# Read-back order and the start of z's job in a one-core block with two linear-attention branches

## The chip, the cores and the metric

The kernel runs on one core of a Trainium2 chip. The metric is the device time of one execution in microseconds (us), as the median of several runs; less is better.

## The reference

One layer, sequence 256, model width 2048, all in float32. From the normalised and modulated input h a wide projection gives the inputs of two branches, and their results are merged, projected and followed by a gated feed-forward block:

```
h    = rms_norm(x) * (1 + scale_m) + shift_m          # 256 x 2048; scale, shift from c @ ada_w
proj = h @ w_in                                       # q,k,v,o of branch A; q|k|v, z of branch B; gates
# branch B: 16 heads of 128, both directions, chunks of 64, gated delta rule
a_mat = I + beta_i * (k k^T) * decay_strict           # per chunk, unit lower triangular
t_mat = inverse(a_mat)                                # triangular solve
u, w  = t_mat @ (beta v), t_mat @ (beta exp(g) k)
...                                                   # recurrence over the chunks -> o_b
y_b   = (rms_norm(o_b) * silu(z)) @ w_branch_b
x     = x + gate_m * ((g_a*y_a + g_b*y_b) @ w_out)
x     = x + gate_f * SwiGLU(norm(x)) ; out = rms_norm(x)
```

## The kernel before

Every large product is made from split weights. A weight tile `raw` (128 x 2048, 1 MB) is loaded by the SyncE queue; ScalarE copies half of it rounded to fp32r (`wh`, 128 x 1024), VectorE makes the rest (`wl = raw - wh`), and TensorE sums three products, `wh*hh`, `wh*hl` and `wl*hh` (`hh`, `hl` are the same split of h). There are three buffers each of `raw`, `wh` and `wl`. A job (`tjob` for 512 columns, `fjob` for 128) is a generator that yields after each half tile; `fill(n)` takes n steps of the jobs that wait in the list `fills`, so that TensorE has work while branch B's small chains run. In the names below, `wl_z1_2_0` is the wl of z's job for group 1, load 2, half at 0; one half is 12 matmuls of TensorE.

Branch B's 16 heads go in four groups of four (`GRP`). `gdn_phase1(h)` computes a head's gates and decays (`dec`, scans over `al`, the decays loaded from HBM by `decay_load`), and on VectorE the triangles `mi`, `mb` from TensorE's products `ks`. GpSimd stores the 32 x 32 diagonal blocks of `mi` to HBM (four DMAs into `inst_d`) and reads them back rearranged into the rows of `uu`. When the fourth head of a group has been read back, `gdn_invert` inverts all 64 blocks of the group at once on VectorE, 60 instructions in place (`utmp` and `uu`), with a `fill(1)` every few of them; GpSimd stores the inverse to HBM and loads it again as `cg`, from which `gdn_blocks` makes `R` and `X`. `gdn_phase2` uses them for two heads at a time: its first product is `p<-R`, its last transposes are `px`, which ScalarE evicts to `obt`.

The four groups run one after the other. While group g is in phase 2, the projections and phase 1 of group g+1 run in `stream`. At the end of a group, z's job of the next group (`z_job(g + 1)`, 8 halves) is put ahead of the other jobs, and `invert(g + 1)` begins. I call these ends the first, second and third turn: about 435 to 515 us (z1, uu1, head 7), 630 to 705 us (z2, uu2, head 11) and 820 to 895 us (z3, uu3, head 15). Group 0 has its z job before.

What sets the order: each engine and each DMA queue works strictly down its own list, and the framework makes these lists from the program with a scheduler. Instructions wrapped in `order(...)` keep their place in the program among each other; others may be taken earlier or later. In `tjob`, the argument `early` is the number of halves that are split before the job's first products, and wherever it is not 0, all `wh` and `wl` of that job are wrapped in `order`. DMAs of GpSimd are on GpSimd's list, with the small `memset` of `al`.

Of the kernel before, what the change touches and what calls it, by code (L numbers as in the profile page):

```python
# [21 lines left out]
NH_B, DK_B = 16, 128  # L22
# [3 lines left out]
GRP = 4  # L26
# [26 lines left out]
def hybrid_block(ctx: ExitStack, tc: tile.TileContext, xr, nfr, crow, pk_d, cst_d, ada2, ada4, win0, winb, wint, wba, wbb, wo, wgu, wd, out, dbg=None):  # L53
# [3 lines left out]
    def pool(stack, name, bufs=1, **kw):  # L57
        return stack.enter_context(tc.tile_pool(name=name, bufs=bufs, **kw))
# [12 lines left out]
    def order(ins, yes=True):  # L71

        return tc.keep_in_program_order(ins) if yes else ins
# [33 lines left out]
    def add():  # L107

        part, b, raw = asked.pop(0)
        c = part * KB + b  # L110
        order(V.scalar_tensor_tensor(raw, raw, 1.0, row_c[:, :D], ALU.mult, ALU.mult, accum_out=mod[:, c : c + 1]), room[0][3] > 1)  # L111
        if b == KB - 1:
            c = slice(part * KB, part * KB + KB)
            V.tensor_tensor(mod[:, c], mod[:, c], pk[:, PK_ADAB + c.start : PK_ADAB + c.stop], ALU.add)
# [31 lines left out]
    def settle(keep=0, only=None):  # L146

        now = [f for f in behind if only is None or f.__name__ == only]
        for f in now[: len(now) - keep]:
            behind.remove(f)  # L150
            f()
# [111 lines left out]
    fills = []  # L263

    def fill(n=1):

        while n and fills:
            if next(fills[0], None):
                n -= 1
            else:  # L270
                fills.pop(0)
# [26 lines left out]
    heads, parts = {}, {}  # L298
# [11 lines left out]
    def decay_load(h):  # L310
        al = als[h] = fr.tile([P, 2, T + 8], F32, tag="al", bufs=2, name=f"al{h}")
        order(G.memset(al[:, :, 0:8], 0.0))
        order(G.dma_start(al[:, :, 8:], alpha_d[:, h].partition_broadcast(P)))
# [48 lines left out]
    def z_job(g, early=0):  # L362
        def done(ps):
            szs[g] = evp.tile([P, 2, 512], F32, tag="sz", bufs=1, name=f"sz{g}")
            for t in range(2):
                S.activation(szs[g][:, t], ps[t], AF.Silu)
        return tjob(f"z{g}", [wint[g, u] for u in range(4)], hh, hl, done, early)
# [121 lines left out]
    with ExitStack() as s0:  # L489
# [72 lines left out]
        zj = z_job(0, 3)  # L562
# [20 lines left out]
    def gdn_phase1(h):  # L583
# [62 lines left out]
        g, hl_ = divmod(h, GRP)  # L646
# [5 lines left out]
                inst[4 * b : 4 * b + 4].rearrange("x j i -> j x i"), mi[32 * b : 32 * b + 32, :, 32 * b : 32 * b + 32]  # L652
            ), b)

        if h + 2 < NH_B:
            decay_load(h + 2)
        order(G.dma_start(uus[g][16 * hl_ : 16 * hl_ + 16], inst))

        cc = ccs[h % NB]

# [43 lines left out]
    def gdn_blocks(g):  # L704

        cg = bk.tile([P, 2, 512], F32, tag="uu", bufs=1, name=f"cg{g}")
        for b in range(4):
            G.dma_start(cg[32 * b : 32 * b + 32, 0], inv_d[g][:, b].rearrange("j x i -> j (x i)"))
        yield
        order(V.transpose(cg[:, 1], cg[:, 0]))  # L710
        F_, Bt, Ft, B_ = (cg[:, i // 2, (i % 2) * 256 : (i % 2 + 1) * 256].rearrange("p (m c) -> p m c", m=8) for i in range(4))

        def mix(dst, a, ca, b, cb):
            order(V.tensor_scalar(dst, b, cb, None, ALU.mult))
            order(V.scalar_tensor_tensor(dst, a, ca, dst, ALU.mult, ALU.add))

        mix(R[:, 0], Ft, even, Bt, odd)
        mix(R[:, 1], B_, even, F_, odd)
        yield
        for i, ab in enumerate(((Ft, Bt), (B_, F_))):  # L720
            for b in range(4):
                r = slice(32 * b, 32 * b + 32)
                order(S.activation(X[r, i, :, b % 2], ab[b // 2][r], AF.Copy))
            yield
        for i, a in enumerate((F_, B_)):
            for b in range(4):
                r = slice(32 * b, 32 * b + 32)
                if i:
                    order(V.tensor_copy(UL[r, i, :, r], a[r]))
                else:  # L730
                    order(S.activation(UL[r, i, :, r], a[r], AF.Copy))
            yield
# [139 lines left out]
    def stream(h0):  # L872

        todo = []

        def piece():

            for q in list(todo):
                q[0] -= 1
                if not q[0]:  # L880
                    todo.remove(q)
                    next(heads1[q[1]])

        for h in range(h0, min(h0 + 2, NH_B)):
            for j in range(3):
                for _ in b_job(h, j):
                    piece()
                    yield True
            todo += [[2, h], [4, h]]
        while todo:  # L890
            fill(1)
            piece()
            yield True
        while True:
            fill(1)
            yield True
# [3 lines left out]
    def mlstm(h):  # L900
# [84 lines left out]
        yield  # L985

    heads1 = {h: gdn_phase1(h) for h in range(NH_B)}
    after = (0, 1, 2, 1, 2, 2, 2, 2, 4, 0)
    last = (0, 1, 2, 1, 2, 2, 1, 1, 3, 0)
# [13 lines left out]
    def invert(g):  # L1003
        gen = gdn_invert(g)
        next(gen)
        fill(4 if g else 6)
        for _ in gen:
            fill(1)

    invert(0)  # L1010
    for g in range(4):
        blocks = gdn_blocks(g)
        next(blocks)
        fill(8)
        next(blocks)
        fill(1)
        pairs = [gdn_phase2(g, p) for p in range(2)]
        if g == 3:
            settle()
            sf.close()  # L1020
            mq["pool"] = pool(sq_, "mq", side="right")
            first2 = [mlstm(h) for h in range(2)]
            for c in first2:
                next(c)
        every[0] = (4, 2, 2, 2)[g]
        for p in range(2):
            pieces = stream(4 * g + 2 * p + 4)
            for n in range(1, 10):

                held[0] = n < 4  # L1030
                if p == 0:
                    next(blocks, None)
                if n == 9 and p and g < 3:

                    zj = z_job(g + 1, int(4 * g + 7 in heads))
                    if 4 * g + 7 in heads:
                        next(zj)
                next(pairs[p], None)
                if g == 3 and n == (8, 4)[p]:
                    next(first2[p])  # L1040
                for _ in range(last[n] if g == 3 else second[n] if p else after[n]):
                    next(pieces)
            for _ in pairs[p]:
                pass

            if g < 3:
                while 4 * g + 2 * p + 5 not in heads:
                    next(pieces)
        if g < 3:
            fills.insert(0, zj)  # L1050
            every[0] = owed[0] = 0
            if asked:
                add()
            invert(g + 1)
# [483 lines left out]
```

## Time and profile before

| | |
|---|---|
| three runs | 2067.28 us median, 2060.01 to 2068.92 |
| profiled execution | 2064.07 us, span 2062.1 us |
| granted TensorE clock, mean | 0.993 |
| TensorE busy | 2019.9 us |
| VectorE / ScalarE / GpSimd busy | 1397.8 / 1027.7 / 116.8 us |
| branch B, heads and groups | from about 160 to 1000 us of the span |

A busy TensorE is the rule throughout, so the views to read are the waits of TensorE, and what each of the three turns looks like on the engines that feed it. "Idle before" in a row is the time in which that engine stood, and behind the arrow is what ended it.

### The profile page before, as it was taken

The numbers are of one execution on the slowest core, as the hardware profiler recorded it, in microseconds if no ns is written. First come the engines' busy times: TensorE is split into PE (matmuls) and PEld (weight loads), VectorE is DVE, ScalarE is ACT, GpSimd is POOL, SyncE is SP. The second block draws the span as 40 slices with busy tenths as digits, with TensorE's granted clock in tenths as the row PEclk, the third lists the DMA queues.
The fourth block names the chain that finished last, engine by engine and source line by source line (L and its number), as shares of the span: only waits on it lengthen the run. The fifth ranks groups of instructions, "written<-read, shape, count | busy, mean of one in ns | idle before, by whom it ended". The sixth has DMA issues, their size and how long they took to land.

```text
span 2062.1 us, 27024 instructions
## 1 busy us (share of the span) xinstructions
PE 2019.9 (98%) x10386; PEld 1697.9 (82%) x10386; DVE 1397.8 (68%) x2062; ACT 1027.7 (50%) x1540; POOL 116.8 (6%) x211
## 2 busy tenths in 40 slices
PE   8999999999999999999999999999999999999998
PEld 6878789978997889789787888788888888878886
DVE  5778877867878788866577778756565655455554
ACT  3146647755665577454534444644444444444443
POOL 0001210111001010110100000200000000000000
PEclk9999999999999999999999999999999999999999
DMA  9986666646666767586776878466766665555553
GB/s 401 420 334 208 193 228 225 215 124 218 227 206 207 241 213 244 189 291 250 258 278 249 321 283 296 157 232 232 255 225 226 251 237 184 187 201 191 197 189 137
DMA packets 78962, 485.64 MB, mean 236 GB/s; under 512 B 10585, under 2 KB 15969, under 8 KB 24433
## 3 DMA queue, kind: packets, MB, share of 16 engines
q1 hardware_dynamic: 63360, 450.95, 60.4%
q0 software_dynamic: 8160, 17.88, 4.0%
q10 hardware_dynamic: 7314, 15.10, 1.9%
q8 instruction: 81, 1.33, 0.3%
q14 instruction: 47, 0.39, 0.1%
HBM read 467.07 MB, written 16.82 MB: 235 GB/s over the span
## 4 chain that ended last, share of the span: by engine, by line
PE 85%; DMA 6%; DVE 6%; ACT 1%; issue 1%; POOL 0%; ACTq 0%; SPq 0%; DVEq 0%; POOLq 0%
PE acc_gt L230 4%; PE acc_gt L232 4%; PE acc_gt L231 4%; PE acc_up L232 4%; PE acc_up L230 4%; PE acc_up L231 4%; PE acc_d L231 4%; PE acc_d L230 4%; PE acc_d L232 4%; DMA ra<-ada 3%; PE acc_o L230 3%; PE acc_o L232 3%; PE acc_o L231 3%; PE acc_b L187 2%; PE acc_b L188 2%; PE acc_b L189 2%
## 5 line engine op out<-in xcount | busy, mean ns | idle before, releaser
L211 DVE TENSOR_TENSOR wl_d<-raw_d,wh_d 128x1024 fp32r<-128x1024 f32 x88 | 107.8, 1225 | 119.9 <-ACT wh_d L209 119.9
L211 DVE TENSOR_TENSOR wl_up<-raw_up,wh_up 128x1024 fp32r<-128x1024 f32 x88 | 107.7, 1225 | 111.3 <-ACT wh_up L209 111.2
L211 DVE TENSOR_TENSOR wl_gt<-raw_gt,wh_gt 128x1024 fp32r<-128x1024 f32 x88 | 108.1, 1229 | 89.2 <-ACT wh_gt L209 89.2
L187 PE MATMUL acc_b<-hh,wh_b 128*128 128x256 f32 x576 | 164.8, 286 | 0.0
L209 ACT ACTIVATE wh_d<-raw_d 128x1024 fp32r<-128x1024 f32 x88 | 93.3, 1061 | 138.9 <-PE acc_d L231 134.0
L189 PE MATMUL acc_b<-hh,wl_b 128*128 128x256 f32 x576 | 160.9, 279 | 0.0
L188 PE MATMUL acc_b<-hl,wh_b 128*128 128x256 f32 x576 | 159.7, 277 | 0.0
L209 ACT ACTIVATE wh_gt<-raw_gt 128x1024 fp32r<-128x1024 f32 x88 | 93.3, 1060 | 128.7 <-PE acc_gt L231 77.3
L111 DVE SCALAR_TENSOR_TENSOR ada<-ada,crow 128x2048 f32<-128x2048 f32 x64 | 146.1, 2282 | 10.2 <-DMA ada<-ada 10.2
L209 ACT ACTIVATE wh_up<-raw_up 128x1024 fp32r<-128x1024 f32 x88 | 93.2, 1060 | 118.1 <-PE acc_up L231 84.2
L230 PE MATMUL acc_gt<-wh_gt,hfh 128*128 128x512 f32 x352 | 139.0, 395 | 0.0
L231 PE MATMUL acc_gt<-wh_gt,hfl 128*128 128x512 f32 x352 | 138.2, 393 | 0.0
L232 PE MATMUL acc_gt<-wl_gt,hfh 128*128 128x512 f32 x352 | 137.4, 390 | 0.0
L230 PE MATMUL acc_up<-wh_up,hfh 128*128 128x512 f32 x352 | 136.9, 389 | 0.0
L231 PE MATMUL acc_up<-wh_up,hfl 128*128 128x512 f32 x352 | 136.9, 389 | 0.0
L232 PE MATMUL acc_up<-wl_up,hfh 128*128 128x512 f32 x352 | 136.9, 389 | 0.0
L230 PE MATMUL acc_d<-wh_d,ffh 128*128 128x512 f32 x344 | 134.3, 391 | 0.0
L231 PE MATMUL acc_d<-wh_d,ffl 128*128 128x512 f32 x344 | 134.3, 390 | 0.0
L232 PE MATMUL acc_d<-wl_d,ffh 128*128 128x512 f32 x344 | 133.9, 389 | 0.0
L557 PE MATMUL first<-x,raw 128*128 128x256 f32 x512 | 115.9, 386 | 6.3 <-ACT x L551 6.3
L557 PEld LDWEIGHTS first<-x,raw 128*128 128x128 f32 x512 | 97.3, 192 | 25.0 <-ACT x L551 11.9
L187 PEld LDWEIGHTS acc_b<-hh,wh_b 128*128 128x128 f32 x576 | 108.5, 188 | 1.2 <-issue 0.9
(373 smaller groups left out, 5261.3 us busy)
## 6 DMA issues: line engine op xcount, KB each, us to landing
ada<-ada SPq DMA_DIRECT2D x64, 1024.0 KB, 5.0
raw_gt<-wgu SPq DMA_DIRECT2D x44, 1024.0 KB, 4.9
raw_up<-wgu SPq DMA_DIRECT2D x44, 1024.0 KB, 4.9
raw_d<-wd SPq DMA_DIRECT2D x44, 1024.0 KB, 4.8
raw_b<-winb SPq DMA_DIRECT2D x36, 1024.0 KB, 5.1
ra<-ada SPq DMA_DIRECT2D x32, 1025.0 KB, 15.2
raw<-win SPq DMA_DIRECT2D x16, 1024.0 KB, 14.5
raw_z<-wint SPq DMA_DIRECT2D x16, 1024.0 KB, 5.4
```

The costliest lines, as they stand in the source:

```text
L111: order(V.scalar_tensor_tensor(raw, raw, 1.0, row_c[:, :D], ALU.mult, ALU.mult, accum_out=mod[:, c : c + 1]), room[0][3] > 1)
L187: PE.matmul(o, wh[:, k], hh[:, kk], start=kk == 0, stop=False)
L188: PE.matmul(o, wh[:, k], hl[:, kk], start=False, stop=False)
L189: PE.matmul(o, wl[:, k], hh[:, kk], start=False, stop=kk == KB - 1)
L209: order(S.activation(wh, raws[u][:, k0 : k0 + 2], AF.Copy), early)
L211: order(V.tensor_tensor(wl, raws[u][:, k0 : k0 + 2], wh.bitcast(F32), ALU.subtract), early)
L230: order(PE.matmul(ps[t], xh[:, kk, c], wh[:, k], start=kk == 0, stop=False), early and steps > 1)
L231: PE.matmul(ps[t], xl[:, kk, c], wh[:, k], start=False, stop=False)
L232: PE.matmul(ps[t], xh[:, kk, c], wl[:, k], start=False, stop=kk == last)
L557: PE.matmul(first[o], raw[:, o], x[:, b], start=b == 0 and o % 2 == 0, stop=b == KB - 1 and o % 2 == 1)
```

## The change

Two edits. For the last head of a group, GpSimd's DMA that reads the triangles back into `uu` is put ahead of the memset and DMA that load the decays of the head after next (heads 3, 7 and 11; the last head, 15, loads no decays any more). And z's job is no longer started ahead of its turn: before, `zj` was made at step 9 of the second pair with `early` 1 and its first `next` split the first half; now it is made when it is put into `fills`, with `early` 0, so it splits its first weights itself, and its `wh` and `wl` are no longer wrapped in `order`.

```diff
@@ gdn_phase1
-        if h + 2 < NH_B:
+        final = hl_ == GRP - 1
+        if h + 2 < NH_B and not final:
             decay_load(h + 2)
         order(G.dma_start(uus[g][16 * hl_ : 16 * hl_ + 16], inst))
+        if h + 2 < NH_B and final:
+            decay_load(h + 2)
@@ loop over the groups
-                if n == 9 and p and g < 3:
-
-                    zj = z_job(g + 1, int(4 * g + 7 in heads))
-                    if 4 * g + 7 in heads:
-                        next(zj)
                 next(pairs[p], None)
@@
         if g < 3:
-            fills.insert(0, zj)
+            fills.insert(0, z_job(g + 1))
             every[0] = owed[0] = 0
```

What it moves in the engines' lists, at three places. On GpSimd at the first turn (`inst_d1`, `uu1`: store and read-back of head 7's triangles; `al9`: decays of head 9), before and after:

```order
L651 DMA inst_d1_119<-mi7_3700 32x4x32 x4
L312 MEMSET al9_3723 128x2x8
L313 DMA al9_3723<-alpha_d_92 128x2x256
L657 DMA uu1_2779<-inst_d1_119 16x1024
L681 DMA inv_d1_123<-uu1_2779 16x16x32 x8
```
```order
L651 DMA inst_d1_119<-mi7_3700 32x4x32 x4
L658 DMA uu1_2779<-inst_d1_119 16x1024
L312 MEMSET al9_3724 128x2x8
L313 DMA al9_3724<-alpha_d_92 128x2x256
L684 DMA inv_d1_123<-uu1_2779 16x16x32 x8
```

The read-back moved ahead of the memset and the decay load, and nothing else changes on GpSimd; groups 0 and 2 look alike.

On VectorE at the first turn, from the last of head 7's triangles to the start of the inversion (`dec8`: decays of head 8), before, and then after, from the sums that precede the triangles:

```order
L645 STREAM_TRANSPOSE mi7_3700<-mb7_3701 128x256
L211 TENSOR_TENSOR wl_z1_0_0_3730<-raw_z1_0_3727,wh_z1_0_0_3729 128x1024
...
L211 TENSOR_TENSOR wl_z1_0_2_3765<-raw_z1_0_3727,wh_z1_0_2_3764 128x1024
L211 TENSOR_TENSOR wl_z1_1_0_3783<-raw_z1_1_3780,wh_z1_1_0_3782 128x1024
L211 TENSOR_TENSOR wl_z1_1_2_3799<-raw_z1_1_3780,wh_z1_1_2_3798 128x1024
L593 SCALAR_TENSOR_TENSOR dec8_4611<-al8_3487,cst_75 128x128
L684 MEMSET uu1_2779 64x32
...
L695 TENSOR_TENSOR uu1_2779<-uu1_2779,utmp1_3749 64x27x4
L211 TENSOR_TENSOR wl_z1_2_0_3826<-raw_z1_2_3823,wh_z1_2_0_3825 128x1024
```
```order
L211 TENSOR_TENSOR wl_z1_0_0_3743<-raw_z1_0_3740,wh_z1_0_0_3742 128x1024
...
L211 TENSOR_TENSOR wl_z1_0_2_3765<-raw_z1_0_3740,wh_z1_0_2_3764 128x1024
L211 TENSOR_TENSOR wl_z1_1_0_3783<-raw_z1_1_3780,wh_z1_1_0_3782 128x1024
L635 SCALAR_TENSOR_TENSOR mi7_3700<-ks7_0_3704,sm7_3690,dec7_3641 128x128
...
L645 STREAM_TRANSPOSE mi7_3700<-mb7_3701 128x256
...
L211 TENSOR_TENSOR wl_z1_1_2_3799<-raw_z1_1_3780,wh_z1_1_2_3798 128x1024
L593 SCALAR_TENSOR_TENSOR dec8_4611<-al8_3487,cst_75 128x128
L211 TENSOR_TENSOR wl_z1_2_0_3826<-raw_z1_2_3823,wh_z1_2_0_3825 128x1024
L211 TENSOR_TENSOR wl_z1_2_2_3848<-raw_z1_2_3823,wh_z1_2_2_3847 128x1024
L687 MEMSET uu1_2779 64x32
```

Three of z's wl moved ahead of the triangles, and the fifth and sixth ahead of the inversion's first instruction. ScalarE's wh moved with them: the first three stand ahead of `obt` and of the copies `cc` of the triangles, where before it was one.

On ScalarE at the third turn (`vv15`: scaled values of head 15; `obt`: eviction of group 2's last transposes; `cc3`: copies of the triangles), before and after:

```order
L621 ACTIVATE vv15_7668<-vps15_7589,nn15_7662 128x128
L209 ACTIVATE wh_z3_0_0_7697<-raw_z3_0_7695 128x1024
L664 ACTIVATE cc3_1163<-mi15_7671 32x2x32
...
L830 ACTIVATE obt10_7711<-px_2_1_7531,pk_74 128x256
L830 ACTIVATE obt11_7714<-px_2_1_7531,pk_74 128x256
...
L209 ACTIVATE wh_z3_0_2_7733<-raw_z3_0_7695 128x1024
```
```order
L621 ACTIVATE vv15_7668<-vps15_7589,nn15_7662 128x128
L833 ACTIVATE obt10_7699<-px_2_1_7531,pk_74 128x256
L833 ACTIVATE obt11_7702<-px_2_1_7531,pk_74 128x256
...
L209 ACTIVATE wh_z3_0_0_7711<-raw_z3_0_7709 128x1024
L667 ACTIVATE cc3_1163<-mi15_7671 32x2x32
...
L209 ACTIVATE wh_z3_0_2_7733<-raw_z3_0_7709 128x1024
```

Here z's first wh moved the other way, behind both `obt`. At the second turn the first three wh stand ahead of `obt` as at the first, and the second and third wl come right behind the first, ahead of the scans `dec`.

## The prediction

> **What bounds the kernel now.** I read the page first, then the list of what TensorE waits for, then the stretches in which it waits. The first row below is the page's busy time, the others the whole run's waits (us in total, times, longest).
>
> ```profile
> PE 2019.9 (98%) x10386; PEld 1697.9 (82%) x10386; DVE 1397.8 (68%) x2062; ACT 1027.7 (50%) x1540; POOL 116.8 (6%) x211
> ...
> PE acc_z L232 <- DVE wl_z L211: 9.8, 10, 2.5
> ...
> PE acc_z L230 <- ACT wh_z L209: 1.7, 2, 0.9
> ```
>
> TensorE is busy for 98%, so the end moves only by its waits and by its clock. Its largest wait is for z's split weights, 11.5 us in all, and the change touches just these. The next table goes by stretches around the first turn (z1) and, last row, the third (z3).
>
> ```profile
> core 0: us, PE busy (x) PEld busy (x) DVE busy (x) ACT busy (x) POOL busy (x), PEclk, DMA share, GB/s
> ...
> 443.00:446.40 3.40, 1.50 (x7) 1.24 (x7) 3.40 (x8) 3.33 (x8) 2.35 (x6) 1.00 0.32 91
> 446.40:449.80 3.40, 3.40 (x9) 2.61 (x8) 3.40 (x4) 1.20 (x2) 1.11 (x2) 0.50 0.59 53
> ...
> 456.60:460.00 3.40, 0.91 (x5) 0.43 (x4) 3.13 (x11) 1.06 (x1) 0.00 (x0) 1.00 0.17 70
> 460.00:463.40 3.40, 3.40 (x9) 2.62 (x10) 3.22 (x8) 0.00 (x0) 0.00 (x0) 0.51 0.00 0
> ...
> 825.00:828.70 3.70, 2.19 (x10) 1.14 (x8) 3.70 (x12) 3.23 (x10) 0.74 (x2) 1.00 0.11 35
> ```
>
> After a stretch in which TensorE worked 1.50 or 0.91 of 3.40 us, its granted clock is 0.50 and 0.51 for the next 3.4 us. That costs 3.4 x (0.50 + 0.49) = 3.4 us on top of the idle time. After 2.19 of 3.70 us it stayed at full speed.
>
> **First turn (z1): why it waits.** TensorE, VectorE and ScalarE in order of time (start us, us; in brackets the idle time before):
>
> ```profile
> 439.31 0.39 PE L231 MATMUL acc_mb<-wh_mb,hl 128*128 128x512 f32 x1
> ...
> 441.84 0.48 PE L230 MATMUL acc_z<-wh_z,hh 128*128 128x512 f32 x1
> ...
> 444.92 0.73 PE L232 MATMUL acc_z<-wl_z,hh 128*128 128x512 f32 x2 [1.90 <-DVE wl_z L211]
> ...
> 459.82 0.60 PE L232 MATMUL acc_z<-wl_z,hh 128*128 128x512 f32 x1 [2.49 <-DVE wl_z L211]
> ...
> 513.49 0.97 PE L746 MATMUL p<-R,cc 128*128 128x32 f32 x8
> ```
> ```profile
> 440.83 0.35 DVE L635 SCALAR_TENSOR_TENSOR mi<-ks,sm,dec 128x128 f32<-128x128 f32 x1 [4.44 <-PE ks L630]
> ...
> 443.68 1.18 DVE L211 TENSOR_TENSOR wl_z<-raw_z,wh_z 128x1024 fp32r<-128x1024 f32 x1
> ...
> 456.60 0.17 DVE L689 TENSOR_TENSOR utmp<-uu 64x30 f32<-64x30 f32 x1 [6.52 <-issue]
> ...
> 458.56 1.21 DVE L211 TENSOR_TENSOR wl_z<-raw_z,wh_z 128x1024 fp32r<-128x1024 f32 x1
> ...
> 466.12 0.37 DVE L689 TENSOR_TENSOR utmp<-uu 64x220 f32<-64x220 f32 x1
> 466.52 0.38 DVE L695 TENSOR_TENSOR uu<-uu,utmp 64x220 f32<-64x220 f32 x1
> ...
> 491.37 0.18 DVE L695 TENSOR_TENSOR uu<-uu,utmp 64x30 f32<-64x30 f32 x1
> ...
> 506.95 0.48 DVE L715 SCALAR_TENSOR_TENSOR R<-cg,cst,R 128x256 f32<-128x256 f32 x1
> ```
> ```profile
> 435.17 1.05 ACT L209 ACTIVATE wh_z<-raw_z 128x1024 fp32r<-128x1024 f32 x1
> 442.12 0.84 ACT L830 ACTIVATE obt<-px,pk 128x256 f32<-128x256 f32 x2 [5.89 <-PE px L826]
> ...
> 453.93 1.06 ACT L209 ACTIVATE wh_z<-raw_z 128x1024 fp32r<-128x1024 f32 x1 [1.69 <-PE acc_z L231]
> 456.68 1.06 ACT L209 ACTIVATE wh_z<-raw_z 128x1024 fp32r<-128x1024 f32 x1 [1.69 <-PE acc_z L231]
> ```
>
> z's first wl stood behind head 7's triangles and came at 443.68. The wait of 2.49 us has another cause: VectorE stood 6.52 us until the triangles had been read back into uu, and z's fifth wl was queued behind that (456.60, then 458.56).
>
> **First turn after the change.** ScalarE and VectorE now split z's first three half loads before the triangles, in time that stood idle (5.89 and 4.44 us). The third needs the buffer that `mb` frees at 439.31 + 0.39 = 439.7: wh to 440.8, wl to 442.0. So the triangles start 1.2 us later than at 440.83; that is the price. The wait of 1.90 us goes. z's fifth and sixth wl stand ahead of uu now and need only buffers that TensorE frees: the 2.49 us go too, and with both the half clock. Removed: 4.4 + 3.4 = 7.8 us.
>
> What is late next? TensorE then needs a new split pair each 2.75 us (453.93 to 456.68) from 441.84 on without a pause. The read-back decides where VectorE's inversion stands. The GpSimd rows, and the times from issue to landing of four read-backs (of 447.97, 641.89, 832.07 and 810.30, in this order):
>
> ```profile
> 446.27 0.73 POOL L313 DMA_DIRECT2D al<-alpha_d  x1
> 447.97 0.52 POOL L657 DMA_DIRECT2D uu<-inst_d  x1 [0.97 <-DMA inst_d<-mi]
> ...
> 832.07 0.51 POOL L657 DMA_DIRECT2D uu<-inst_d  x1 [1.95 <-DMA inst_d<-mi]
> ```
> ```profile
> uu<-inst_d POOLq DMA_DIRECT2D x1, 64.0 KB, 8.6
> ...
> uu<-inst_d POOLq DMA_DIRECT2D x1, 64.0 KB, 6.3
> ...
> uu<-inst_d POOLq DMA_DIRECT2D x1, 64.0 KB, 5.3
> ...
> uu<-inst_d POOLq DMA_DIRECT2D x1, 64.0 KB, 3.6
> ```
>
> The read-back is not issued sooner by its new place: it waits for the store of the triangles (0.97 us even behind the decay load, 1.95 without one). The gain is in the landing: 8.6 and 6.3 us with the decay load in front, 5.3 and 3.6 for heads 15 and 14, which have none. I take 5.3, because the next weight load (`raw_mb`) will run beside it as `raw_z` did at 832; bounds 3.6 and 8.6. Hence uu at 447.97 + 1.2 + 5.3 = 454.5 instead of 456.6. The decay load then lands some 4 us later and nobody waits: head 9 reads it a group later.
>
> By the Trainium skill (DMA: Bandwidth & Descriptors, Queues, rings and completion order) each DMA engine goes round-robin between queue rows, a packet at a time. The trace agrees for the read-backs beside a 1 MB load, which still land in 5.3 us; that rule alone would leave 5.3 where it is.
>
> From 454.5 I count VectorE's rows in the new order, 0.42 us for a long inversion step (466.12 to 466.52) and 1.13 for a wl. Most wl are in time. Twice nine steps stand between two wl, 3.8 us against 2.75: ahead of `wl_mb1_3_0` TensorE waits about 0.8 us, ahead of `wl_o1_1_0` 0.5. So 7.8 - 1.3 = 6.5 us are left. The inversion ends near 489.3 (one wl fewer in it), 2 us before 491.4, so R's first half comes near 505 instead of 507.4; TensorE comes to p at 513.5 - 6.5 = 507.0. It passes, with 2 us to spare. Bounds: 7.8 us, and 2.0 with the landing at 8.6, when the wl queued behind uu are 3.3 us late and a half-clock stretch may return.
>
> **Second turn (z2).** Waits between 625 and 670 us, then a piece of the chain:
>
> ```profile
> PE acc_z L230 <- ACT wh_z L209: 1.7, 2, 0.9
> PE acc_z L232 <- DVE wl_z L211: 1.2, 3, 0.5
> ```
> ```profile
> 642.99 7.49 DMA raw_z<-wint
> ```
>
> 2.9 us. The third load of z2 could start only when `wl_z2_0_2` had freed its buffer (642.99). That wl now comes right behind the first, near 639.9, so the load lands 3 us sooner. Given back: about 0.4 at `wl_z2_2_0`, behind uu, and 1.3 where nine inversion steps stand ahead of `wl_ma2_2_2`. Net 1.2 us, bounds 0 and 2.9.
>
> **Third turn (z3).** No decay load here; only the order of ScalarE differs, and it is worse at the start.
>
> ```profile
> PE acc_z L232 <- DVE wl_z L211: 3.2, 4, 1.6
> ```
> ```profile
> 824.92 1.05 ACT L209 ACTIVATE wh_z<-raw_z 128x1024 fp32r<-128x1024 f32 x1
> ```
> ```profile
> 825.39 0.60 PE L826 MATMUL px<-cst,on 128*128 128x128 f32 x4
> ...
> 828.82 0.73 PE L232 MATMUL acc_z<-wl_z,hh 128*128 128x512 f32 x2 [1.60 <-DVE wl_z L211]
> ```
>
> wh_z3_0_0 ran at 824.92, ahead of obt. Now it stands behind both obt, which wait for px (to 826.0): obt to 827.1, wh to 828.2, wl to 829.3. TensorE stands from 826.0 to 828.2 and comes to its first wl 0.6 us later than at 828.82. The other three waits (3.2 - 1.6 = 1.6 us) go, since `wl_z3_2_0` moves ahead of the inversion's first sum. Clock: the new idle of 2.2 us lies between the 1.90 and 2.49 us that were followed by half clock, so I charge 1.7 us. Net 1.6 - 0.6 - 1.7 = -0.7 us, a loss; bounds +1.6 and -2.3.
>
> The Trainium skill (TensorE: Matmul & The Clock Gate, Part 1) says that activity is judged in free-running windows of 3413 ns; the two slow stretches, 3.4 us long, agree. By that rule an idle of 2.2 us is not always punished: it depends on where a window's edge falls. Without that charge the third turn gains 1.0.
>
> Head 3's read-back moves too, but TensorE waits for no z and no R there: nothing.
>
> **Sum.** 6.5 + 1.2 - 0.7 = 7.0 us. The profiled execution took 2064.07 us, so 2057.1; it lies 3.2 below the median of the runs, 2067.28, and measured by that I predict 2060 us. The runs go from 2060.01 to 2068.92 with nothing changed, so about 0.5% (10.3 us) is what can be told from no change.
>
> **Rivals.**
> - *All of it goes.* The wl are in time everywhere and the clock holds: 7.8 + 2.9 + 1.0 = 11.7 us, 2056. For it: only 1.3 and 1.7 us of lateness, by a count of rows; against it, VectorE is busy 3.22 of 3.40 us while it inverts.
> - *The clock holds at the third turn* (by the Trainium skill's windows): if an edge cuts the 2.2 us into pieces of less than the 1.60 that went unpunished, 1.7 us stay: 8.7 in all, 2058.6. For it: edges of unknown place; against: 1.90 was enough.
> - *The read-back lands no sooner* (weight loads were the cause of 8.6, not the decay load): first turn 2.0, second 1.0, third -0.7, 2.3 us in all: 2065. For it: 6.3 lies between; against: 3.6 and 5.3.
> - *Slower.* The read-back, 1.2 us late by the triangles' new place, meets `raw_mb` and lands so late that wl and R hold TensorE. Each us beyond 5.3 costs about one at the first turn; the gain of 7.0 is used up from a landing of 12.3 us on. At 15 us: 2070. The slowest row here is 8.6, so this is unlikely.
>
> **Chances.** Forecast 0.40, clock holds 0.22, all goes 0.20, no sooner 0.13, slower 0.05. Faster by over 0.5% needs 10.3 us: most of the third case and a lucky tenth of the first two, 0.24. Slower by over 0.5%: under the last case, 0.03. Range: from 2056 to 2065, widened by some 3 to 5 us for the scatter of the runs: 2051 to 2068.
>
> **What would show it.** First turn: no TensorE wait over 1 us ahead of 465, clock 1.00 in 446 to 464, `mi` about 1.2 us behind ks, read-back landing near 5 us. Second: raw_z2_2 issued near 640. Third: wh_z behind obt, TensorE idle over 2 us there, perhaps half clock behind it. At p no wait. I am wrong if TensorE waits for R, or if the read-back still lands in 8 us.

## The result and the profile after

| | before | after |
|---|---|---|
| median of 11 runs each, us | 2067.28 (2060.01 to 2068.92) | 2055.47 (2048.52 to 2058.71) |
| ratio | 1 | 0.9946, 95% interval 0.9934 to 0.9958 |
| profiled execution, us | 2064.07 | 2058.71 |
| its span, us | 2062.1 | 2056.7 |
| TensorE busy, us | 2019.9 | 2018.3 |

The change gains 0.54%, 11.8 us by the medians; forecast were 7.0 us and 2060. The two profiled executions are only 5.4 us apart, the one after being the highest of its eleven runs, so one pair of profiles doesn't show it all. Below stand three profiles of the changed kernel and two of the one before. One of the twelve runs of experiment 4's second kernel took 3430 us at a granted clock of 0.58; its ratio leaves that run out, and without it its median is 2061.28 us.

What TensorE waits for in the whole run, after (us in total, times, longest):

```profile
PE vps L601 <- ACT vf L337: 4.3, 4, 3.6
...
PE acc_z L230 <- ACT wh_z L209: 2.5, 1, 2.5
...
PE acc_ma L232 <- DVE wl_ma L211: 1.8, 1, 1.8
...
PE acc_z L232 <- DVE wl_z L211: 1.1, 1, 1.1
```

The row of 9.8 us for `wl_z` has shrunk to one wait of 1.1, in z0's job, which the change doesn't touch. New are 2.5 us ahead of z3 and 1.8 us at `wl_ma2_2_2`. Between 425 and 480 us TensorE waits for nothing. The stretches of the first turn and of the third, after:

```profile
core 0: us, PE busy (x) PEld busy (x) DVE busy (x) ACT busy (x) POOL busy (x), PEclk, DMA share, GB/s
443.00:446.40 3.40, 3.40 (x17) 2.78 (x16) 3.11 (x9) 2.69 (x7) 1.83 (x4) 1.00 0.27 82
446.40:449.80 3.40, 3.40 (x17) 2.78 (x16) 2.42 (x3) 1.33 (x2) 1.64 (x4) 1.00 0.50 128
456.60:460.00 3.40, 3.40 (x16) 2.78 (x16) 3.23 (x9) 1.06 (x1) 0.00 (x0) 1.00 0.30 67
460.00:463.40 3.40, 3.40 (x17) 2.78 (x16) 3.30 (x6) 2.86 (x3) 0.00 (x0) 1.00 0.66 272
821.80:825.20 3.40, 1.15 (x4) 0.67 (x4) 2.59 (x7) 2.83 (x8) 1.69 (x4) 0.99 0.27 84
825.20:828.60 3.40, 3.34 (x9) 2.61 (x9) 1.97 (x3) 2.37 (x4) 0.99 (x2) 0.51 0.07 13
```

The first turn is busy throughout at full clock. The third has the idle time and the half clock behind it that the prediction charged. VectorE and GpSimd at the first turn and TensorE at its end, after:

```profile
441.35 0.35 DVE L635 SCALAR_TENSOR_TENSOR mi<-ks,sm,dec 128x128 f32<-128x128 f32 x1
443.84 0.44 DVE L645 STREAM_TRANSPOSE mi<-mb 128x256 f32<-128x256 f32 x1
...
453.01 0.19 DVE L692 TENSOR_TENSOR utmp<-uu 64x30 f32<-64x30 f32 x1 [1.16 <-DMA uu<-inst_d]
...
486.48 0.18 DVE L698 TENSOR_TENSOR uu<-uu,utmp 64x30 f32<-64x30 f32 x1
...
499.46 0.49 DVE L718 SCALAR_TENSOR_TENSOR R<-cg,cst,R 128x256 f32<-128x256 f32 x1
```
```profile
448.50 0.52 POOL L658 DMA_DIRECT2D uu<-inst_d  x1 [1.75 <-DMA inst_d<-mi]
449.00 0.13 POOL L312 MEMSET al<- 128x16 f32 x1
449.05 0.74 POOL L313 DMA_DIRECT2D al<-alpha_d  x1
```
```profile
504.44 0.97 PE L749 MATMUL p<-R,cc 128*128 128x32 f32 x8
```

uu is there at 453.0 instead of 456.6, the inversion ends at 486.7 instead of 491.6, and TensorE comes to p at 504.4 instead of 513.5. R's first half is ready at 499.95, so 4.5 us are to spare.

The table that the rest rests on divides each profiled execution at the first `p<-R` of each group, that is at the end of each turn (us):

| kernel, profile | p0 to p1 (first turn) | p1 to p2 (second) | p2 to p3 (third) | p3 to the end |
|---|---|---|---|---|
| before, first and second | 191.0, 190.6 | 192.3, 196.6 | 188.9, 190.4 | 1167.4, 1164.6 |
| after, first, second and third | 181.7, 182.4, 181.8 | 195.9, 194.4, 192.8 | 189.3, 188.3, 189.4 | 1167.0, 1167.1, 1167.7 |

The gain is 8.8 us in the first turn (means 190.8 and 182.0). In these means the second turn gains 0.1 us, the third 0.6, and 1.3 are lost behind p3, but within one kernel the second turn differs by 3 to 4 us from profile to profile, so these small differences can't be told from nothing.

### The profile page after: what moved, and what is told of

The parts are those of the page before. It is cut to its first block, busy times and chain, and to the rows that moved or that the text cites. A ratio compares the mean times of both kernels' runs of the same rounds, so it can differ in the third digit from the quotient of the medians.

```text
span 2056.7 us, 27025 instructions
## 1 busy us (share of the span) xinstructions
PE 2018.3 (98%) x10386; PEld 1699.9 (83%) x10386; DVE 1398.0 (68%) x2062; ACT 1027.4 (50%) x1540; POOL 116.9 (6%) x211
## 4 chain that ended last, share of the span: by engine, by line
PE 85%; DMA 6%; DVE 5%; ACT 2%; issue 1%; POOL 0%; ACTq 0%; SPq 0%; DVEq 0%; POOLq 0%
PE acc_gt L230 4%; PE acc_gt L232 4%; PE acc_gt L231 4%; PE acc_up L230 4%; PE acc_up L231 4%; PE acc_up L232 4%; PE acc_d L230 4%; PE acc_d L232 4%; PE acc_d L231 4%; PE acc_o L232 3%; PE acc_o L230 3%; PE acc_o L231 3%; DMA ra<-ada 2%; PE first L557 2%; PE acc_b L187 2%; PE acc_b L188 2%
## 5 line engine op out<-in xcount | busy, mean ns | idle before, releaser
L557 PEld LDWEIGHTS first<-x,raw 128*128 128x128 f32 x512 | 97.3, 192 | 24.8 <-ACT x L551 11.8
```

The lines of the kernel that those rows point to most:

```text
L557: PE.matmul(first[o], raw[:, o], x[:, b], start=b == 0 and o % 2 == 0, stop=b == KB - 1 and o % 2 == 1)
```

## The experiments

**1. The read-back's new place alone, and 2. z's job alone.** The first is the diff's hunk in `gdn_phase1` on the kernel before, the second the hunks in the group loop:

```diff
 # 1: before, with
+        final = hl_ == GRP - 1
+        if h + 2 < NH_B and not final: decay_load(h + 2)
         order(G.dma_start(uus[g]..., inst))
+        if h + 2 < NH_B and final: decay_load(h + 2)
 # 2: before, with
-                if n == 9 and p and g < 3: zj = z_job(g + 1, ...); ...
-            fills.insert(0, zj)
+            fills.insert(0, z_job(g + 1))
```

> Before with the read-back's new place alone. Theory A (each edit takes away one of the two waits of the first turn, with the half-clock stretch behind it): the read-back lands some 3 us sooner, the wait of 2.49 us for z's fifth wl goes and with it 1.7 us of half clock, the wait of 1.90 us stays: 4.2 us below before, about 2063. Theory B (z's job alone carries the gain, the read-back only lands sooner): no change, 2067, and the wait of about 2.5 us is still there.

> After with the decay load back in front of the read-back: z's job alone. Theory A: uu comes at about 457 us of the span instead of 453, and the seventh wl of z1, which stands in the inversion behind uu's first steps, is some 3 us late, so TensorE waits again for about 2 to 3 us, with a half-clock stretch behind it: 3 to 5 us above after, 2059 to 2061. Theory B: no wait over 1 us in the first turn, as fast as after, 2055.5.

Measured: read-back alone 2060.38 us, ratio 0.9971 (0.9960 to 0.9982); z's job alone 2059.02, 0.9965 (0.9953 to 0.9977). On the same chip after ran in 2052.58, so z's job alone lies 6.4 us above it, more than the expected 3 to 5. First turn 186.3 and 186.0 us, so 4.5 and 4.8 below before (190.8), 9.3 together against 8.8 with both: within the noise they add up. TensorE's waits in the first turn, read-back alone and then z's job alone:

```profile
444.11 0.74 PE L232 MATMUL acc_z<-wl_z,hh 128*128 128x512 f32 x2 [1.91 <-DVE wl_z L211]
455.68 0.51 PE L232 MATMUL acc_z<-wl_z,hh 128*128 128x512 f32 x1 [0.44 <-DVE wl_z L211]
462.11 0.51 PE L232 MATMUL acc_z<-wl_z,hh 128*128 128x512 f32 x1 [0.34 <-DVE wl_z L211]
```
```profile
459.76 0.50 PE L232 MATMUL acc_z<-wl_z,hh 128*128 128x512 f32 x1 [0.93 <-DVE wl_z L211]
472.93 0.50 PE L232 MATMUL acc_mb<-wl_mb,hh 128*128 128x512 f32 x1 [1.70 <-DVE wl_mb L211]
```

The first keeps the wait of 1.91 us and loses that of 2.49. The second loses both, but uu comes at 457.40, so the wl that stand within the inversion are late: `wl_z1_3_0` (0.93) and `wl_mb1_3_0` (1.70). Theory B, that z's job alone carries the gain, is out. The start of the inversion with z's job alone:

```profile
457.40 0.17 DVE L689 TENSOR_TENSOR utmp<-uu 64x30 f32<-64x30 f32 x1 [5.14 <-issue]
```

This also gives the price of a late read-back: uu is 4.4 us later than after (457.40 against 453.01), the first turn 4.0 us longer (186.0 against 182.0), so here about 0.9 us for each us.

**3. Place or freedom of z's job.** Once the job is made in its turn, but its wh and wl are held in program order; once it is made ahead of its turn as before, with only its first half held. Both have the read-back's new place:

```diff
 # held: after, with
+            pin = early or name in ("z1", "z2", "z3")
-            order(S.activation(wh, ...), early); ...
+            order(S.activation(wh, ...), pin); ...
 # first half held: experiment 1, with
-        def halves(u, k0):
+        def halves(u, k0, early=early):
-            wh, wl = made.pop(0) if made else halves(u, k0)
+            wh, wl = made.pop(0) if made else halves(u, k0, 0 if name in ('z1', 'z2', 'z3') else early)
```

> After, but all wh and wl of z1, z2 and z3 held in program order as before: z's job starts in its turn without being free. Theory F (the gain of the z edit comes from the freedom to be split ahead of the triangles and ahead of uu): the wait of about 1.9 us in the first turn is back, and longer, since wh now stands behind obt; only the read-back's gain is left, 2060 to 2063, 7 to 10 us above after. Theory P (it is the place at which the job is made): as fast as after, 2053.

> Before with the read-back's new place, z's jobs made ahead of their turn as before, but only the first half held in order; the other halves are free. Theory F: z's fifth and later wl stand ahead of uu or early in the inversion, but the first stands behind the triangles, so the wait of 1.9 us stays in the first turn, and the third turn has 1.6 instead of 2.5: about as fast as after or 1 to 2 us above it, 2053 to 2055. Theory P: only the read-back's gain, 2060.

Measured: all held 2062.39 us, 0.9987 (0.9978 to 0.9995); first half held 2056.40, 0.9960 (0.9946 to 0.9973). TensorE's longest wait in the first turn, all held and then first half held:

```profile
444.38 0.79 PE L231 MATMUL acc_z<-wh_z,hh 128*128 128x512 f32 x1 [2.51 <-ACT wh_z L210]
```
```profile
445.21 0.73 PE L232 MATMUL acc_z<-wl_z,hh 128*128 128x512 f32 x2 [1.90 <-DVE wl_z L211]
```

The first turn took 186.6 and 186.1 us, as with the read-back's new place alone (186.3), and 4 us more than after (182.0). All held, z's job in its turn gains nothing there, since wh now stands behind obt, at all three turns, 2.51 us each time; in the whole kernel about half of the read-back's gain is left (0.13% below before instead of 0.29%, on different chips). So the place as such brings nothing; theory F holds. Freedom of the later halves, with the first still behind the triangles, leaves the 1.90: what gains in the first turn is that z's first halves pass in front of head 7's triangles. The second kernel came out 1.4 us above its expected 2053 to 2055.

**4. Why the read-back landed late.** The decay load of a group's last head goes to ScalarE's DMA queue, first ahead of the read-back and then behind the copies cc, so as to be under way beside it:

```diff
 # both on the kernel before
-        order(G.dma_start(al[:, :, 8:], ...))
+        order(eng.dma_start(al[:, :, 8:], ...))
 # ahead:  decay_load(h + 2, S if hl_ == GRP - 1 else G) ahead of the read-back
 # beside: decay_load(h + 2, S) as the last line of corners(), for the last head
```

> Before with the decay load of a group's last head issued from ScalarE's DMA queue instead of GpSimd's, ahead of the read-back as before; nothing else differs. If the read-back lands late because the decay load stands in front of it in the same queue: landing near 4.5 us at the first turn as with the read-back's new place, and 4 to 6 us below before, about 2060. If it is the decay load's traffic beside the read-back, whatever its queue: landing near 8.5 us as before, and no change, 2065.

> Before with the decay load of a group's last head issued from ScalarE's DMA queue behind the copies cc, at about 446 us, so that it is under way beside the read-back but in another queue; the read-back has nothing in front of it. If the place in GpSimd's queue made the read-back late: landing 4 to 5.5 us at the first turn, 2 to 4.5 at the second, and 5 to 8 us below before. If the decay load's traffic did: landing over 7 us at both turns, and 0 to 2 us below before.

Measured: ahead 2058.99 us, 0.9962 (0.9947 to 0.9976); beside 2061.82, 0.9982 (0.9970 to 0.9995). Issue to landing of the triangles' store and of the read-back at the first turn, for after, then the read-back with the decay load ahead in the other queue, then store and read-back with the decay load beside:

```profile
inst_d<-mi POOLq DMA_DIRECT2D x4, 16.0 KB, 1.7
uu<-inst_d POOLq DMA_DIRECT2D x1, 64.0 KB, 4.3
```
```profile
uu<-inst_d POOLq DMA_DIRECT2D x1, 64.0 KB, 5.3
```
```profile
inst_d<-mi POOLq DMA_DIRECT2D x4, 16.0 KB, 4.0
uu<-inst_d POOLq DMA_DIRECT2D x1, 64.0 KB, 3.7
```

With the decay load directly in front in the same queue the read-back took 8.6, 8.5 and 8.4 us (two profiles of before, z's job alone), and at the second turn 6.3, 8.9 and 7.2 against 3.7, 3.7 and 4.5 in the three profiles of after. Both kernels take something out of the first turn: 186.8 and 187.3 us, against 190.8 before. Ahead gained more by the medians (8.4 us against before on its chip) than either theory gave it, beside about 4 us, between the two theories. And neither kernel separates queue from traffic as it was meant to. Ahead, the decay load was issued at 433.71, 13 us before the read-back. Beside, it was issued at 442.76, earlier than expected, and met the store instead; at the second turn it had landed (634.73 + 4.6) before the read-back was issued (640.62). In the second, a small DMA beside the decay load came late even from another queue: the store landed in 4.0 us, and GpSimd waited 3.46 us for it instead of 1.74 with the read-back's new place alone:

```profile
449.23 0.52 POOL L658 DMA_DIRECT2D uu<-inst_d  x1 [3.46 <-DMA inst_d<-mi]
```

So the decay load, issued directly in front, is the cause of the late landing: in every profile without it directly in front, the read-back of the first turn landed in 2.4 to 5.3 us. That its traffic alone delays a small DMA rests on this one profile, and a late store isn't proof of it: at the second turn the third profile of after has a wait of 3.45 us for the store with no decay load beside it. How much of the 4 us is the place in the queue stays open.

**5. The third turn.** z3's first half is made ahead of its turn again, and only it is held; then the same with that half made one step sooner:

```diff
 # after, with halves() as in experiment 3, and
+                if n == 9 and p and g == 2:        # sooner: within n == 8, ahead of its third piece
+                    zj = z_job(3, 1)
+                    next(zj)
-            fills.insert(0, z_job(g + 1))
+            fills.insert(0, zj if g == 2 else z_job(g + 1))
```

> After, with z3's first half alone split ahead of its turn as before (held in program order; the other halves stay free). ScalarE's wh then stands ahead of obt again. By the prediction's third turn: the wait of 2.5 us for wh becomes one of about 1.6 us for wl, and the half clock behind it goes: 0.6 to 0.9 plus 1.7, so 2.3 to 2.6 us below after, about 2053. If what the third turn loses is made up later, or the half clock falls there anyway: within 1 us of after.

> The version of the third turn once more, beside the changed kernel on the same chip, since the first pair (2051.09 and 2052.58) does not tell them apart. If the third turn's loss, worked out as 2.3 to 2.6 us, counts in full: 2 to 3 us below after. If the half clock falls on the third turn in either version, as in both first profiles: 0.6 to 0.9 us below.

> The version of the third turn (z3's first half split ahead) with that half made a step sooner, within step 8 of the second pair: its wl stands ahead of head 15's triangles. The wait of 1.60 us there goes, and the half clock that stands behind it at times: 1.6 to 3 us below that version, 2048 to 2050. Rival: the half holds one of the three wh and wl buffers longer, so TensorE waits for the second half of a2's weights instead, over 1.5 us, and nothing is gained.

Measured: 2051.09 us, 0.9932 (0.9919 to 0.9944), and again 2053.91, 0.9939 (0.9923 to 0.9955); sooner 2052.36, 0.9938 (0.9924 to 0.9951). Beside the first two on the same chips after ran in 2052.58 and 2056.17; beside the last it did not run. From p2 to p3 the profiles show 187.8 and 187.0, and 185.6 sooner, against a mean of 189.0 after; sooner, TensorE waits for nothing between 800 and 850 us. So the profiles are 1.2 to 3.4 us shorter there, but the intervals overlap: none of these is shown to beat the changed kernel. The rival of the last one (a2's second half late) did not come true; its wait in the second turn was 2.08 us for a wl of z2, of which the cause was not followed.

**6. Both kernels again, for more profiles.** No edit.

> The changed kernel once more, for a second profile and as the yardstick on this chip: ratio 0.994 to 0.996. TensorE's waits should be the same within 0.3 us each. If the clock is judged in windows that run on their own, the half-clock stretches, in the first profile behind 557, 588, 663, 823 and 1305 us, come partly at other places or in other number, and the profiled time differs by 1.7 us for each; if each idle of over 1.9 us is punished wherever it lies, they come at the same five places.

> The changed kernel a third time, as the yardstick for the version of the third turn and for a third profile: ratio 0.993 to 0.995, the wait of 2.5 us ahead of z3, no wait over 1 us in the first turn, first p of the second group 182 us behind that of the first.

> The kernel before once more, for a second profile. Ratio 1. If the first profile is typical, TensorE's waits are the same within 0.5 us each, and the span less the half-clock loss is within 1 us of the first one's. If the first profile was a favourable one (its pair shows 5.4 us of gain where the medians show 11 to 13), the second one has longer waits ahead of z's weights or a later landing of the read-back.

Measured: after 2052.58 us, 0.9934 (0.9921 to 0.9946), and 2056.17, 0.9939 (0.9918 to 0.9959); before 2066.24, 1.0003 (0.9994 to 1.0012).

In after, between 100 and 2000 us, the half clock came partly at other places: from about 559, 590, 665, 825 and 1306 us in the first profile, from 560, 591, 823, 990 and 1304 in the second, from 558, 988, 1067 and 1306 in the third. So not every idle of over 1.9 us is punished: the 2.51 us ahead of z3 stand in all three profiles, and the third has no half clock behind them. That the waits are the same within 0.3 us holds for that one (2.51 three times), but not for vps (3.60, 3.08 and 3.51) or `wl_ma2_2_2` (1.83, 1.79 and 0.46).

Before, second profile, TensorE's waits in the first turn and the second:

```profile
443.97 0.74 PE L232 MATMUL acc_z<-wl_z,hh 128*128 128x512 f32 x2 [1.90 <-DVE wl_z L211]
458.82 0.50 PE L232 MATMUL acc_z<-wl_z,hh 128*128 128x512 f32 x1 [3.72 <-DVE wl_z L211]
...
639.72 0.73 PE L232 MATMUL acc_z<-wl_z,hh 128*128 128x512 f32 x2 [1.28 <-DVE wl_z L211]
642.76 0.50 PE L232 MATMUL acc_z<-wl_z,hh 128*128 128x512 f32 x1 [0.24 <-DVE wl_z L211]
652.83 0.50 PE L230 MATMUL acc_z<-wh_z,hh 128*128 128x512 f32 x1 [2.24 <-ACT wh_z L209]
655.17 0.80 PE L232 MATMUL acc_z<-wl_z,hh 128*128 128x512 f32 x1 [1.60 <-DVE wl_z L211]
```

The first turn is as long as in the first profile (190.6 against 191.0), though the 1.90 was not followed by half clock this time: TensorE just came earlier to the wait for uu, 3.72 instead of 2.49. Here, half clock ahead of a wait on another engine cost nothing of its own. The second turn's waits add up to 5.4 us instead of 2.9, with 3.4 us of half clock behind them: the first profile of before was a favourable one, and the expectation that the waits are the same within 0.5 us was wrong.

## Why the prediction was right, and where its steps were off

**First turn, forecast 6.5 us, measured 8.8.** The mechanism is as forecast. Measured from z's first product, the triangles start 1.1 us later (441.35 with the product at 441.22, instead of 440.83 with 441.84); the read-back is issued no sooner (448.50, with a wait of 1.75 us for the store) and lands sooner; the waits of 1.90 and 2.49 us and the half clock are gone. Mis-sized is the term "given back", 1.3 us: no wait ahead of `wl_mb1_3_0` or `wl_o1_1_0` in any of the three profiles. The landing was 4.3, 4.3 and 4.6 us, not 5.3, so uu came at 453.0 instead of 454.5. With uu at 457.40 (z's job alone) just that wait appears, 1.70 us. The removed 7.8 us don't reach 8.8 either; about 0.5 us of the rest is a slower pace of the matmuls in both profiles of before (last section).

**Second turn, forecast 1.2, measured 0.1** (means of p1 to p2 194.5 and 194.4) **as the difference of two larger terms.** Within the turn, from z2's first product to p, 68.2 and 72.3 us became 67.6, 66.2 and 65.4: 3.8 gained. The third load of z2 comes 3.1 us sooner (2.4 instead of 5.5 us behind z2's first product), as forecast, and the nine inversion steps ahead of `wl_ma2_2_2` cost 1.83, 1.79 and 0.46 us, forecast 1.3. But between the first turn's end and z2 124.0 and 124.3 us became 128.3, 128.1 and 127.3: 3.8 given back at a place for which the sum had no term. TensorE comes 9 us sooner to vps of head 8 and waits longer there, before and then after:

```profile
567.21 0.44 PE L601 MATMUL vps<-cst,vf 128*128 128x128 f32 x2 [2.75 <-ACT vf L337]
```
```profile
559.20 0.69 PE L601 MATMUL vps<-cst,vf 128*128 128x128 f32 x2 [3.60 <-ACT vf L337]
```

On ScalarE vf stands behind a wh that waits for its weight load, after:

```profile
557.78 1.06 ACT L182 ACTIVATE wh_a<-raw_a 128x1024 fp32r<-128x1024 f32 x1 [5.16 <-DMA raw_a<-winb]
```

The load is issued 9 us sooner too, but it takes 7.4, 6.7 and 7.2 us from its issue to that wh instead of 6.3 and 6.7; why is open. The wait grew by 0.1 to 0.9 us, but the half clock behind it took 3.4 to 5.1 us (with a second wait 29 us on) instead of 1.7. A gain turned into a new wait and, mostly, into clock.

That is no fixed price of the change. The kernels of experiment 5 have the same order as after on VectorE, ScalarE and GpSimd up to p2, and in the first profile of the version of the third turn no half clock follows the same wait:

```profile
558.23 0.44 PE L601 MATMUL vps<-cst,vf 128*128 128x128 f32 x2 [2.58 <-ACT vf L337]
```

From the first turn's end to z2 it took 122.4 us, less than before, and its second turn 188.0; the other two took 192.2 and 193.0. Over all six profiles with this order the second turn is 192.7 us on average, 1.8 below before, which is near the forecast 1.2, but with a scatter of 188.0 to 195.9. The first turn of the three was 182.0, 184.5 and 182.1 us.

**Third turn, forecast a loss of 0.7, measured a gain of 0.6** (means of p2 to p3; 188.9 and 190.4 before, 188.3 to 189.4 after, so the sign isn't certain). The order shows as forecast: TensorE stands 2.51 us for wh behind obt in all three profiles (estimated 2.2), and the later waits are gone, 3.0 us from z3's first product to p even with the half clock (68.65 became 65.63). The half clock of 1.7 us came in two profiles and not in the third.

**Head 3 and the decay load, forecast nothing.** Right: the first p of group 0 stands at 322.5 and 322.4 before, 322.7, 322.6 and 322.6 after, and nobody waits for al.

**The rivals.** "All of it goes" (2056) came nearest in time: its wl are in time at the first turn, but not at the second, and its clock doesn't hold. "The read-back lands no sooner" and "slower" are out by the landings of 4.3 to 4.6 us. The charge for the clock was wrong in its premise: I took 1.60 us of idle as spared and 1.90 as punished. Two stretches each of read-back alone (an idle of 1.91, spared), of the version of the third turn (1.60, punished) and of the third profile of after (2.51, spared) show otherwise (the stretch with the idle time, then the next):

```profile
442.00:445.40 3.40, 1.49 (x7) 1.08 (x7) 3.40 (x8) 3.33 (x9) 2.16 (x4) 1.00 0.29 87
445.40:448.80 3.40, 3.35 (x15) 2.46 (x14) 3.40 (x4) 1.39 (x2) 1.31 (x4) 1.00 0.37 63
```
```profile
813.30:816.70 3.40, 1.76 (x10) 1.00 (x8) 3.30 (x10) 2.93 (x9) 0.91 (x2) 1.00 0.02 5
816.70:820.10 3.40, 3.40 (x9) 2.62 (x10) 1.74 (x2) 2.25 (x4) 1.45 (x4) 0.52 0.35 96
```
```profile
819.00:822.40 3.40, 0.89 (x6) 0.63 (x5) 2.59 (x10) 2.26 (x5) 0.87 (x2) 1.00 0.26 87
822.40:825.80 3.40, 3.35 (x14) 2.17 (x12) 1.96 (x2) 3.33 (x8) 1.66 (x4) 1.00 0.11 19
```

Over all the profiles taken, half clock followed 3 of the 8 idles of 1.6 us ahead of z3's first wl, 4 of the 6 of 1.90 us in the first turn, and 5 of the 7 of 2.51 us for wh. So the right term for an idle of 1.6 to 2.5 us is a chance of 1.7 us, not the 1.7 themselves. The Trainium skill (TensorE: Matmul & The Clock Gate, Part 1) says that the windows run on their own; the three pairs of stretches above agree.

**The sum, forecast 7.0.** The profiles give 8.1 us and the medians 11.8. Only the first turn's term is shown by experiments. That the profiles come so near to the sum is partly luck: against the forecast, 2.3 us more were gained in the first turn, about 1 us less in the second and 1.3 more in the third, and 1.3 were lost behind p3, where the sum had nothing. The 2055.47 lie 4.5 us below the forecast 2060, inside a range that had been widened for the scatter of the runs.

**What stays open.** The profiles give 8.1 us on average (spans of 2062.1 and 2064.5 against 2056.7, 2054.7 and 2054.3), the medians 11 to 13. The profiled executions of after lie high in their series (the highest of 11, the highest of 6, the fourth of 6 from below), and the first of before low. Part of the missing 3 to 5 us may be clock. Where both kernels ran on the same chip, the mean granted clock is 0.9932 before (17 runs) and 0.9943 after (6 runs), on another chip 0.9928 (11) and 0.9938 (6): about 2 us of the time each. Single runs of after differ by more than that: the fastest of the eleven, 2048.52 us, had 0.996, the profiled one, 2058.71, had 0.992, which is 8 of the 10 us between them. What the rest is, the profiles taken don't show.

## What to carry to other kernels

A small DMA that a chain waits for goes in front of a larger one that nobody waits for, even where it cannot be issued sooner: here that was worth 4 us of landing at once. Whether the gains of two edits on the same stretch add up shows only when they are tested one by one and together: here 4.5 and 4.8 us alone, 8.8 together. And follow the gain past its stretch, since the next weight load or an idle TensorE's clock can take part of it back, here 50 us later.

## What the runs showed of the hardware

A TensorE that the profile shows as busy can be put to half clock. The kernel before around its 24 `pden` matmuls of one column each, and their row:

```profile
992.80:996.20 3.40, 3.40 (x28) 3.19 (x26) 1.31 (x2) 1.06 (x1) 0.00 (x0) 0.97 0.75 224
996.20:999.60 3.40, 3.40 (x11) 2.82 (x12) 0.59 (x6) 0.24 (x2) 0.70 (x1) 0.50 0.52 183
999.60:1003.00 3.40, 3.40 (x10) 2.67 (x9) 0.04 (x1) 1.06 (x1) 1.88 (x4) 0.53 0.99 337
```
```profile
993.80 3.13 PE L947 MATMUL pden<-ones,mdec 128*128 128x1 f32 x24
```

No wait stands there, and 3.4 us are lost (3.4 x (0.03 + 0.50 + 0.47)); in the second profile of before and in the second and third of after 1.7 us are lost at this place, and in the first profile of after the clock held.

The pace of equal matmuls has two levels at a granted clock of 1.00, each for a whole stretch: 22 matmuls of 128x256 take 2.59 us before the first turn's end (118 ns each) and 2.49 us after (113). First and last of them, before and then after:

```profile
509.83 0.28 PE L189 MATMUL acc_a<-hh,wl_a 128*128 128x256 f32 x1
...
512.42 0.28 PE L187 MATMUL acc_a<-hh,wh_a 128*128 128x256 f32 x1
```
```profile
499.79 0.28 PE L188 MATMUL acc_a<-hl,wh_a 128*128 128x256 f32 x1
...
502.28 0.28 PE L189 MATMUL acc_a<-hh,wl_a 128*128 128x256 f32 x1
```

In the second profile of before the 128x512 matmuls of the first turn take 233 ns instead of 229, and in the first profile of the version of the third turn the 128x256 ones 118, so it does not go with the change. What sets it is open.
